# Row gathers of an expert layer: the added wait for a TensorE product taken away

## The chip, the cores and the metric

The kernel runs on one NeuronCore of a Trainium2 chip. The metric is the device time of one execution in microseconds (us), lower is better. Engines are named as in the profile: PE is TensorE (PEld its weight loads), DVE is VectorE, ACT is ScalarE, POOL is GpSimd, SP is SyncE, whose queue issues the plain loads and stores.

## The reference

The program is one layer of a sequence model on 512 tokens of width 2048. Retention and mLSTM mixing come first; the part that matters here is the last one, a "PEER" layer: each token picks 8 x 16 of 16384 experts, and an expert is one row of `peer_down` and one row of `peer_up`.

```
qh = (tb @ w_query).reshape(P_BLOCK, P_HEADS, 2, P_DQ // 2)
...
eid = jnp.take_along_axis(cand_i, best_j, axis=-1)
g = jax.nn.softmax(best_s, axis=-1)
act = jax.nn.gelu(jnp.einsum('thkd,td->thk', expert_down[eid], tb).astype(jnp.float32), approximate=False)
return jnp.einsum('thk,thkd->td', (g * act).astype(tb.dtype), expert_up[eid])
```

## The kernel before, in words

The expert layer is split by token. For 352 tokens (`ND`) it is computed densely on PE: every one of the 16384 experts, in 128 tiles of 128 experts. For the other 160 tokens (`G_` = 128 + 32) it is computed sparsely: rows of the two tables are gathered by index, and DVE multiplies them. The two run side by side in `experts`.

**The dense half.** A hidden tile (`hidden`, line 1187) is `dn[i]` times the activations: two weight loads of 512 KB, 16 products of three matmuls each (`mm3`, line 236; float32 is split into a high and a low part). The first 38 tiles (`NE`) were computed in earlier stages, stored to HBM as `hs` and come back as `hf`. A tile is multiplied by its gates (`gt`, line 1452) and split into high and low (`hh`, lines 233 and 234). Tiles form 16 groups of 8 (`GRP`); after a group, 16 weight loads of `upt` (line 1478 for the first output blocks, line 1494 for the others) give its share of the output (`part`, line 1468), which DVE adds into `acc` (line 1502). Each weight load, of `dn` or `upt`, goes through `weight` (line 224): one DMA into one of 7 `raw` buffers, a cast on ACT (line 228), a subtraction on DVE (line 229) into one of 3 `ws` buffers, and then exactly 24 matmuls of 352 columns. So the stage has 256 + 2 x 90 = 436 such weight steps.

**The sparse half.** There are 320 slots: 128 + 32 rows per token block from `dnr`, and then as many from `up`. `row` (line 1332) takes one slot: `rows` (line 1297) starts an indirect DMA from POOL's queue that gathers 128 rows of 2048 floats into one of three `row` buffers (`ROW_BUFS`), and the DVE operation of the slot two earlier (`LAG`) is emitted: `down` (line 1304, a product with a sum) or `up` (line 1310, multiply and add into `gacc`). `gather` (line 1325) calls `row` so that slots advance evenly with the PE work: `SPAN` is the total of all its arguments, and a slot is taken when its share has been reached.

**What sets the order.** The order in which `experts` emits work is only a priority. The framework's scheduler lays each engine's instructions out by priority and by when it expects their inputs to be ready, and on the chip each engine then runs its own list strictly in order. Weight steps are emitted with a raised priority (`AHEAD`). The gather has one dependency more than its data needs: `self.last` is the last matmul emitted so far, and `add_manual_dep` (line 1301) makes the gather wait for it.

```
            g = G.indirect_dma_start(out=r, out_offset=None, in_=src,
                                     in_offset=bass.IndirectOffsetOnAxis(ap=eid[i][:, s_:s_ + 1], axis=0))
            self.tc.add_manual_dep(g.ins, self.last.ins.name, PACE, reason="pace of the gathers")
```

Of the kernel before, what the change touches and what calls it, by code (L numbers as in the profile page):

```python
# [12 lines left out]
AF = mybir.ActivationFunctionType  # L13
OP = mybir.AluOpType
AX = mybir.AxisListType
PACE = mybir.DependencyInfo(mybir.DependencyClass.Sync, mybir.DependencyReason.DATA)
PSUM = bass.MemoryType.PSUM
DRAM = bass.MemoryType.DRAM

# [138 lines left out]
ND = T - G_  # L158
# [24 lines left out]
class K:  # L183
# [64 lines left out]
    def tjob(self, srcs, targets, nk=KT, order=range(8), one=False):  # L248

        n, last = 0, len(targets) - 1  # L250
        for u, src in enumerate(srcs):
            w = self.weight(src)
            for k8 in order if u else range(8):
                if n == self.LATE:
                    self.flush()
                if n in self.STEPS and self.mixing:
                    next(self.mixing, None)
                c = slice(k8 * P, (k8 + 1) * P)
                for t, (ps, rhs) in enumerate(targets):
                    self.last = self.mm3(ps, (w[:, 0, c], w[:, 1, c]), rhs(u * 8 + k8),  # L260
                                         n == 0 and not (one and t), n == nk - 1 and not (one and t < last))
                n += 1

# [1023 lines left out]
    def experts(self, d2):  # L1287
        a, V, S, TE, SY, G, d0 = self.a, self.V, self.S, self.TE, self.SY, self.G, self.d0
# [3 lines left out]
        eid = [self.eid[0].rearrange("p h k -> p (h k)"), self.eid[1]]  # L1292
# [3 lines left out]

        def rows(src, i, s_):
            r = d2.tile([P, D], F32, name="row", bufs=ROW_BUFS)
            g = G.indirect_dma_start(out=r, out_offset=None, in_=src,  # L1299
                                     in_offset=bass.IndirectOffsetOnAxis(ap=eid[i][:, s_:s_ + 1], axis=0))  # L1300
            self.tc.add_manual_dep(g.ins, self.last.ins.name, PACE, reason="pace of the gathers")
            return r

        def down(i, s_, r):
# [20 lines left out]
        def gather(n):  # L1325

            nonlocal done
            done += n
            while slots and NS - len(slots) < NS * done // SPAN:
                row()  # L1330

        def row():

            if slots:
                f, w, i, s_ = slots.pop(0)
                late.append((f, i, s_, rows(w, i, s_)))
            if len(late) > LAG or not slots:
                f, *x = late.pop(0)
                f(*x)
# [17 lines left out]
        def end0():  # L1357
            nonlocal xg, xh, sqg
            while slots or late:
                row()  # L1360
            t = d2.tile([P, 2, T], F32, name="xs", tag="gt", bufs=2)
            xh, sqg = t[:, 0].rearrange("p (k t) -> p k t", k=KT), t[:, 1]
            xg = d2.tile([P, KT, P], F32, name="xg", tag="row", bufs=ROW_BUFS)
            SY.dma_start(xg, self.X1[:, :, :P].rearrange("k p t -> p k t"))
            SY.dma_start(xh, self.X1[:, :, P:G_].rearrange("k p t -> p k t"))

        def end1():
            t = residuals(NPA)

            def more():  # L1370
                add_residuals(NPA, t)
                t2 = residuals(NPA + 4)
                self.todo.append(lambda: add_residuals(NPA + 4, t2))
            self.todo.append(more)
# [49 lines left out]
        def final(k, ps, x):  # L1424

            V.scalar_tensor_tensor(x2[k], ps[:, :ND], gt2[:, k:k + 1], x, op0=OP.mult, op1=OP.add)
            sq = d2.tile([P, ND], F32, name="sqd", bufs=2) if k else ssd[:, :ND]
            S.activation(sq, x2[k], AF.Square)
            if sqs:
                V.tensor_add(ssd[:, :ND], ssd[:, :ND], sqs.pop())  # L1430
            if k:
                sqs.append(sq)
# [3 lines left out]
        def tile(i):  # L1436

            g, j = divmod(i, 4)
            if j == 0:
                for n in range(len(gts), min(g + 2, P // 4)):  # L1440
                    gts[n] = d2.tile([P, ND // 32, 4, 32], F32, name="gt", bufs=2)
                    SY.dma_start(gts[n].rearrange("p c i t -> p c (i t)"), self.GD[n])
            if i < NE:
                t = d0.tile([P, ND], F32, name="hf", bufs=4)
                SY.dma_start(t, self.HS[i])
            else:
                self.todo.append(lambda: gather(HID // 2))
                t = self.hidden(i)
                gather(HID // 2)
            with self.tc.high_priority(offset=SOON):  # L1450
                tv = t.rearrange("p (c t) -> p c t", t=32)
                V.tensor_tensor(tv, tv, gts[g][:, :, j], OP.mult)
                w = d2.tile([P, 2, ND], F32R, name="hh", tag="hh", bufs=GRP + 1)
                self.split(w[:, 0], w[:, 1], t)
            return w

        hs = []
        for g in range(NG):
            for i in range(len(hs), min(GRP * (g + 1) + FORE, P)):
                if g == NG - 1 and i % GRP == GRP - 3:  # L1460
                    end0()
                    end1()
                elif g == NG - 1 and i % GRP == GRP - 1:
                    self.todo += [end3, end2]
                hs.append(tile(i))
            hh = hs[GRP * g:GRP * (g + 1)]

            def part(w, q, d_, ps, js):

                own = d_ >= NPA  # L1470
                for j in js:
                    c = slice(j * 256 + d_ % 2 * P, j * 256 + (d_ % 2 + 1) * P)
                    i = 4 * q + j
                    self.last = self.mm3(ps[:, :ND], (w[:, 0, c], w[:, 1, c]), (hh[i][:, 0], hh[i][:, 1]),
                                         i == 0 and (own or g == 0), i == GRP - 1 and (own or g == NG - 1))

            for q in range(GRP // 4):
                ws = [self.weight(a["upt"][g, u, q]) for u in range(NPA // 2)]
                for js in (range(3), (3,)) if g == NG - 1 and q == GRP // 4 - 1 else (range(4),):
                    for d_ in range(NPA):  # L1480
                        part(ws[d_ // 2], q, d_, pac[d_], js)
                gather((UP if (g + 1) * GRP > NE else UP0) * NPA // 2 * 4 // GRP)
            if g == NG - 1:
                for d_ in range(NPA):
                    x2[d_] = d0.tile([P, ND], F32, name="hf", bufs=4)
                    final(d_, pac[d_], xd[:, d_])
            for u in range(8):
                if g == NG - 1 and u in END:
                    (end4, end5)[END.index(u)]()
                if u >= NPA // 2:  # L1490
                    ds = (2 * u, 2 * u + 1)
                    pss = [self.ps("upp") for _ in ds]
                    for q in range(GRP // 4):
                        w = self.weight(a["upt"][g, u, q])
                        for d_, ps in zip(ds, pss):
                            part(w, q, d_, ps, range(4))
                            if q < GRP // 4 - 1:
                                continue
                            if g == 0:
                                V.tensor_copy(x2[d_], ps[:, :ND])  # L1500
                            elif g < NG - 1:
                                V.tensor_add(x2[d_], x2[d_], ps[:, :ND])
                            else:
                                final(d_, ps, x2[d_])
                    gather(UP if (g + 1) * GRP > NE else UP0)
        r = self.r2[:, :ND]
# [18 lines left out]
```

## Time and profile before

| | |
|---|---|
| median of 3 runs | 4090.67 us (4087.46 to 4096.19) |
| the profiled execution, its own time | 4075.81 us |
| its span in the trace | 4074.0 us |
| mean granted PE clock, share of full | 0.984 |
| bytes moved by DMA | 979.72 MB, mean 240 GB/s |
| of these by the gathers' queue | 335.56 MB |

Busy shares (PE 97%, DVE 70%, ACT 32%, POOL 11%) are means over the whole program; the dense and sparse halves of the experts run from about 2311 us to 4057 us, and that stretch has to be read by itself. A matmul's busy time overlaps its successor's, so the distance between the starts of two matmuls, not the duration of one, tells what PE needs. A wait is put down to the engine that came last. "DMA share" is the mean busy share of the core's 16 DMA engines.

### The profile page before, as it was taken

The page shows a single profiled execution, that of the slowest core. Times are in us where ns is not written, and L with a number is a line of the kernel's source. Part 1 is how long each engine was busy: PE and PEld are TensorE (multiplying, and loading weights), DVE is VectorE, ACT ScalarE, POOL GpSimd, SP SyncE. Part 2 cuts the span into 40 slices and gives each one's busy share as a digit, 9 for nine tenths or more (in the row PEclk, how much of TensorE's full clock was granted, in tenths as well). Part 3 has the DMA queues.
Part 4 walks back from the last instruction along what each step waited for, and adds up shares of the span by engine and source line. Part 5 has one row for each costly group of instructions (what it writes and reads, how often), then busy time and mean ns, then how long its engine had stood idle before and what let it go on. Part 6 is the DMA issues. An engine that isn't in the chain of part 4 may idle for free.

```text
span 4074.0 us, 56684 instructions
## 1 busy us (share of the span) xinstructions
PE 3950.5 (97%) x22470; PEld 3570.2 (88%) x22470; DVE 2860.3 (70%) x4448; ACT 1324.0 (32%) x1823; POOL 467.0 (11%) x328
## 2 busy tenths in 40 slices
PE   7999999999999999999999999999999999999998
PEld 4788887777788888799999999999999999999998
DVE  7952237677733443488889678888888888898956
ACT  3322124245422222343334333333223323333333
POOL 0000000000000000000000021333223333333300
PEclk7999999999999999999999999999999999999999
DMA  8522237667733444433357889999999999999963
GB/s 305 212 75 86 70 101 255 227 212 251 259 128 113 142 155 145 150 108 110 102 152 222 264 316 334 353 363 375 364 344 364 374 364 370 379 391 379 381 223 104
DMA packets 300539, 979.72 MB, mean 240 GB/s; under 512 B 32368, under 2 KB 101744, under 8 KB 259184
## 3 DMA queue, kind: packets, MB, share of 16 engines
q1 hardware_dynamic: 251888, 636.33, 45.7%
q0 software_dynamic: 46080, 335.56, 20.9%
q8 instruction: 176, 2.88, 0.3%
q10 hardware_dynamic: 2304, 4.20, 0.3%
q14 instruction: 91, 0.75, 0.1%
HBM read 915.63 MB, written 60.33 MB: 240 GB/s over the span
## 4 chain that ended last, share of the span: by engine, by line
PE 57%; DMA 20%; DVE 10%; issue 9%; ACT 1%; POOL 0%; SPq 0%; DVEq 0%; POOLq 0%; ACTq 0%
PE px L240 10%; PE px L238 10%; PE px L239 10%; DMA row<-in_dnr,eid 7%; DMA row<-in_up,eid 6%; PE hid L238 3%; DVE ws L229 3%; PE hid L240 3%; PE hid L239 3%; PE va L239 2%; PE va L238 2%; PE va L240 2%; DMA row<-in_dnr,eidx 2%; DVE gacc L1314 2%; DMA row<-in_up,eidx 2%
## 5 line engine op out<-in xcount | busy, mean ns | idle before, releaser
L229 DVE TENSOR_TENSOR ws<-raw,ws 128x1024 fp32r<-128x1024 f32 x770 | 937.0, 1220 | 608.1 <-ACT ws L228 606.5
L228 ACT CAST ws<-raw 128x1024 fp32r<-128x1024 f32 x770 | 805.6, 1049 | 1697.5 <-PE px L240 567.1
L240 PE MATMUL hid<-h,ws 128*128 128x352 f32 x2048 | 660.8, 323 | 23.5 <-DVE ws L229 23.3
L238 PE MATMUL hid<-h,ws 128*128 128x352 f32 x2048 | 674.5, 329 | 0.7 <-ACT ws L228 0.7
L239 PE MATMUL hid<-h,ws 128*128 128x352 f32 x2048 | 659.5, 322 | 0.0
L1299 POOL DMA_INDIRECT row<-in_dnr,eid x128 | 188.1, 1470 | 2777.6 <-DVE hh L234 2287.6
L238 PE MATMUL upp<-hh,ws 128*128 128x352 f32 x1536 | 499.2, 325 | 0.0
L240 PE MATMUL upp<-hh,ws 128*128 128x352 f32 x1536 | 493.0, 321 | 5.6 <-DVE ws L229 5.6
L239 PE MATMUL upp<-hh,ws 128*128 128x352 f32 x1536 | 493.7, 321 | 0.0
L1305 DVE SCALAR_TENSOR_TENSOR row<-row,h2n 128x2048 f32<-128x2048 f32 x160 | 365.7, 2289 | 92.2 <-DMA row<-in_dnr,eid 68.7
L1314 DVE SCALAR_TENSOR_TENSOR gacc<-row,wts,gacc 128x2048 f32<-128x2048 f32 x158 | 371.0, 2348 | 71.7 <-DMA row<-in_up,eid 56.2
L238 PE MATMUL px<-hhi,ws 128*128 128x512 f32 x1024 | 413.1, 403 | 0.0
L240 PEld LDWEIGHTS hid<-h,ws 128*128 128x128 f32 x2048 | 385.7, 188 | 31.0 <-DVE ws L229 30.7
L240 PE MATMUL px<-hhi,ws 128*128 128x512 f32 x1024 | 407.7, 398 | 0.0
L239 PE MATMUL px<-hlo,ws 128*128 128x512 f32 x1024 | 405.8, 396 | 0.0
L239 PEld LDWEIGHTS hid<-h,ws 128*128 128x128 f32 x2048 | 390.2, 191 | 0.0
L238 PEld LDWEIGHTS hid<-h,ws 128*128 128x128 f32 x2048 | 385.5, 188 | 0.9 <-ACT ws L228 0.9
L240 PEld LDWEIGHTS upp<-hh,ws 128*128 128x128 f32 x1536 | 288.8, 188 | 7.3 <-DVE ws L229 7.2
L239 PEld LDWEIGHTS upp<-hh,ws 128*128 128x128 f32 x1536 | 292.2, 190 | 0.0
L238 PEld LDWEIGHTS upp<-hh,ws 128*128 128x128 f32 x1536 | 288.3, 188 | 0.0
L240 PEld LDWEIGHTS px<-hhi,ws 128*128 128x128 f32 x1024 | 192.5, 188 | 48.1 <-issue 2.9
L239 PEld LDWEIGHTS px<-hlo,ws 128*128 128x128 f32 x1024 | 192.6, 188 | 43.6 <-issue 4.6
(451 smaller groups left out, 6474.5 us busy)
## 6 DMA issues: line engine op xcount, KB each, us to landing
raw<-in_dn SPq DMA_DIRECT2D x256, 512.0 KB
raw<-in_upt SPq DMA_DIRECT2D x256, 512.0 KB
raw<-in_wada_r SPq DMA_DIRECT2D x160, 512.0 KB
raw<-in_wt SPq DMA_DIRECT2D x130, 512.0 KB
gd<-sg SPq DMA_DIRECT2D x11, 2048.0 KB
gt<-gd SPq DMA_DIRECT2D x32, 704.0 KB
raw<-in_wada_s SPq DMA_DIRECT2D x32, 512.0 KB
raw<-in_wn SPq DMA_DIRECT2D x32, 512.0 KB
```

The lines of the kernel that those rows point to most:

```text
L228: self.S.copy(w[:, 0], r)
L229: self.V.tensor_sub(w[:, 1], r, w[:, 0].bitcast(F32))
L238: mm(out, lhsT=l[0], rhs=r[0], start=start, stop=False)
L239: mm(out, lhsT=l[0], rhs=r[1], start=False, stop=False)
L240: return mm(out, lhsT=l[1], rhs=r[0], start=False, stop=stop)
L1299: g = G.indirect_dma_start(out=r, out_offset=None, in_=src, in_offset=bass.IndirectOffsetOnAxis(ap=eid[i][:, s_:s_ + 1], axis=0))
L1305: V.scalar_tensor_tensor(r, r, 1.0, self.h2n[i], op0=OP.mult, op1=OP.mult, accum_out=dots[i][:, s_:s_ + 1])
L1314: V.scalar_tensor_tensor(gacc[i], r, wts[i][:, s_:s_ + 1], gacc[i], op0=OP.mult, op1=OP.add)
```

## The change

The argument that named the last matmul goes, and with it the gather's extra dependency. A gather still waits for its buffer, that is for the DVE operation that read it three slots before.

```
-PACE = mybir.DependencyInfo(mybir.DependencyClass.Sync, mybir.DependencyReason.DATA)
...
-                    self.last = self.mm3(ps, (w[:, 0, c], w[:, 1, c]), rhs(u * 8 + k8),
+                    self.mm3(ps, (w[:, 0, c], w[:, 1, c]), rhs(u * 8 + k8),
...
-            g = G.indirect_dma_start(out=r, out_offset=None, in_=src,
-                                     in_offset=bass.IndirectOffsetOnAxis(ap=eid[i][:, s_:s_ + 1], axis=0))
-            self.tc.add_manual_dep(g.ins, self.last.ins.name, PACE, reason="pace of the gathers")
+            G.indirect_dma_start(out=r, out_offset=None, in_=src,
+                                 in_offset=bass.IndirectOffsetOnAxis(ap=eid[i][:, s_:s_ + 1], axis=0))
...
-                    self.last = self.mm3(ps[:, :ND], (w[:, 0, c], w[:, 1, c]), (hh[i][:, 0], hh[i][:, 1]),
+                    self.mm3(ps[:, :ND], (w[:, 0, c], w[:, 1, c]), (hh[i][:, 0], hh[i][:, 1]),
```

Lines after the removed ones stand one or two numbers lower in the changed kernel (229 becomes 228, 1305 becomes 1303, 1502 becomes 1500).

The first place is POOL's own queue in the stage, which holds nothing but gathers. Before, with the semaphores each waits for (DMASW is the queue's own count, DVE the buffer, PE the product):

```order
L1299 DMA row<-in_dnr,eid 128x2048 [waits DMASW5_49,DVE_49,PE_49]
L1299 DMA row<-in_dnr,eid 128x2048 [waits DMASW6_49,DVE_49,PE_49]
L1299 DMA row<-in_dnr,eid 128x2048 [waits DMASW7_49,DVE_49,PE_49]
L1299 DMA row<-in_dnr,eid 128x2048 [waits DMASW0_49,DVE_49,PE_49]
L1299 DMA row<-in_dnr,eid 128x2048 [waits DMASW1_49,DVE_49,PE_49]
```

The same place now:

```order
L1298 DMA row<-in_dnr,eid 128x2048 [waits DMASW5_49,DVE_49]
L1298 DMA row<-in_dnr,eid 128x2048 [waits DMASW6_49,DVE_49]
L1298 DMA row<-in_dnr,eid 128x2048 [waits DMASW7_49,DVE_49]
L1298 DMA row<-in_dnr,eid 128x2048 [waits DMASW0_49,DVE_49]
L1298 DMA row<-in_dnr,eid 128x2048 [waits DMASW1_49,DVE_49]
```

The wait for PE is gone, the order of the gathers is the same. The second place is DVE's list in the second group's `upt` part. Here `ws` is a weight step, `row,dots` the operation that reads a gathered row, and `acc` the addition of a result of PE. Before:

```order
L229 TENSOR_TENSOR ws<-raw,ws 128x1024 x2
L1502 TENSOR_TENSOR acc<-acc,upp 128x352
L1305 SCALAR_TENSOR_TENSOR row,dots_18631<-row,h2n_11759 128x2048
L1502 TENSOR_TENSOR acc<-acc,upp 128x352
L229 TENSOR_TENSOR ws<-raw,ws 128x1024 x2
L1502 TENSOR_TENSOR acc<-acc,upp 128x352
L1305 SCALAR_TENSOR_TENSOR row,dots_18631<-row,h2n_11759 128x2048
L1502 TENSOR_TENSOR acc<-acc,upp 128x352
```

The same part now:

```order
L1303 SCALAR_TENSOR_TENSOR row,dots_18631<-row,h2n_11759 128x2048
L228 TENSOR_TENSOR ws<-raw,ws 128x1024
L1500 TENSOR_TENSOR acc<-acc,upp 128x352
L1303 SCALAR_TENSOR_TENSOR row,dots_18631<-row,h2n_11759 128x2048
L228 TENSOR_TENSOR ws<-raw,ws 128x1024
L1500 TENSOR_TENSOR acc<-acc,upp 128x352
L1303 SCALAR_TENSOR_TENSOR row,dots_18631<-row,h2n_11759 128x2048
L228 TENSOR_TENSOR ws<-raw,ws 128x1024
```

Where one row operation stood to two weight steps, one stands to each. Counted over DVE's whole list of the stage: the 320th and last row operation stood behind weight step 394 of 436, and now stands behind weight step 320; 100 tiles of `hf` and `hh` and 144 operations on `acc` lie ahead of it, where 121 and 168 did. The third place is the start of the stage on DVE. Before:

```order
L1422 MEMSET ssd 128x32
L229 TENSOR_TENSOR ws<-raw,ws 128x1024 x3
L1452 TENSOR_TENSOR hf<-hf,gt 128x352
L234 TENSOR_TENSOR hh<-hf,hh 128x352
L1452 TENSOR_TENSOR hf<-hf,gt 128x352 x2
```

The same place now:

```order
L1420 MEMSET ssd 128x32
L228 TENSOR_TENSOR ws<-raw,ws 128x1024
L1303 SCALAR_TENSOR_TENSOR row,dots_18631<-row,h2n_11759 128x2048
L228 TENSOR_TENSOR ws<-raw,ws 128x1024
L1303 SCALAR_TENSOR_TENSOR row,dots_18631<-row,h2n_11759 128x2048
L228 TENSOR_TENSOR ws<-raw,ws 128x1024
L1303 SCALAR_TENSOR_TENSOR row,dots_18631<-row,h2n_11759 128x2048
L1450 TENSOR_TENSOR hf<-hf,gt 128x352 x3
L233 TENSOR_TENSOR hh<-hf,hh 128x352 x3
```

Three row operations now stand ahead of the first `hf` and `hh`. PE's list differs only in the first group's first `part`, whose products come in another order; SP's list has the same transfers, some of them a few places earlier or later.

## Rows read from the trace of the kernel before

**Rows 1.** The page: busy time, share and count; DMA share in 40 slices.

```profile
PE 3950.5 (97%) x22470; PEld 3570.2 (88%) x22470; DVE 2860.3 (70%) x4448; ACT 1324.0 (32%) x1823; POOL 467.0 (11%) x328
...
DMA  8522237667733444433357889999999999999963
```

**Rows 2.** Timeline of PE at the stage's first and last matmuls: start us, us, instruction.

```profile
2311.29 0.66 PE L238 MATMUL pac<-hh,ws 128*128 128x352 f32 x1 [6.03 <-ACT hh L233]
...
4056.75 0.32 PE L239 MATMUL upp<-hh,ws 128*128 128x352 f32 x1
4056.91 0.32 PE L240 MATMUL upp<-hh,ws 128*128 128x352 f32 x1
```

**Rows 3.** Windows: stretch, length; busy PE, PEld, DVE, ACT, POOL; clock, DMA share, GB/s.

```profile
2300.00:2600.00 300.00, 293.32 (x1810) 291.86 (x1810) 231.52 (x282) 97.83 (x120) 63.34 (x40) 0.98 0.87 322
2600.00:3900.00 1300.00, 1260.15 (x7745) 1248.51 (x7745) 1135.13 (x1013) 398.09 (x485) 399.22 (x280) 0.99 0.96 371
```

**Rows 4.** Waits from 2320 us on: engine, line, releaser: total us, times, longest.

```profile
POOL row L1299 <- PE upp L240: 350.0, 71, 8.7
POOL row L1299 <- PE hid L240: 177.6, 62, 7.7
POOL row L1299 <- PE pac L240: 176.5, 27, 10.9
POOL row L1299 <- DVE gacc L1314: 131.7, 42, 6.3
...
PE hid L240 <- DVE ws L229: 22.7, 18, 4.0
...
PE pac L240 <- DVE ws L229: 11.7, 9, 3.3
```

**Rows 5.** The page: the gathers' queue, and sizes of the loads.

```profile
q0 software_dynamic: 46080, 335.56, 20.9%
...
raw<-in_upt SPq DMA_DIRECT2D x256, 512.0 KB
...
gt<-gd SPq DMA_DIRECT2D x32, 704.0 KB
...
hf<-hs SPq DMA_DIRECT2D x38, 176.0 KB
```

**Rows 6.** Windows of 50 us, columns as in group 3.

```profile
2700.00:2750.00 50.00, 45.63 (x268) 45.06 (x267) 38.69 (x40) 13.44 (x16) 14.86 (x9) 0.93 0.88 330
...
3350.00:3400.00 50.00, 48.73 (x305) 48.45 (x304) 45.24 (x35) 15.99 (x20) 13.13 (x10) 1.00 0.99 395
...
3650.00:3700.00 50.00, 50.00 (x315) 50.00 (x314) 47.92 (x38) 14.63 (x16) 14.96 (x13) 1.00 0.99 386
```

**Rows 7.** DVE's groups, 2311 to 3890 us: busy us, mean ns; idle before, releasers.

```profile
L229 DVE TENSOR_TENSOR ws<-raw,ws 128x1024 fp32r<-128x1024 f32 x393 | 476.9, 1219 | 31.9 <-ACT ws L228 30.9 <-issue 0.8
L1314 DVE SCALAR_TENSOR_TENSOR gacc<-row,wts,gacc 128x2048 f32<-128x2048 f32 x158 | 371.0, 2348 | 71.7 <-DMA row<-in_up,eid 56.2 <-DMA row<-in_up,eidx 14.6
L1305 DVE SCALAR_TENSOR_TENSOR row<-row,h2n 128x2048 f32<-128x2048 f32 x160 | 365.7, 2289 | 92.2 <-DMA row<-in_dnr,eid 68.7 <-DMA row<-in_dnr,eidx 22.7
L1502 DVE TENSOR_TENSOR acc<-acc,upp 128x352 f32<-128x352 f32 x156 | 80.1, 513 | 0.0
L234 DVE TENSOR_TENSOR hh<-hf,hh 128x352 fp32r<-128x352 f32 x121 | 61.6, 518 | 4.3 <-ACT hh L233 4.0
```

**Rows 8.** Timelines of POOL and DVE: first gather, its product, and the last product.

```profile
2323.21 2.89 POOL L1299 DMA_INDIRECT row<-in_dnr,eid  x1 [2282.44 <-DVE hh L234]
...
2333.74 2.29 DVE L1305 SCALAR_TENSOR_TENSOR row<-row,h2n 128x2048 f32<-128x2048 f32 x1 [3.38 <-DMA row<-in_dnr,eid]
...
3886.46 2.35 DVE L1314 SCALAR_TENSOR_TENSOR gacc<-row,wts,gacc 128x2048 f32<-128x2048 f32 x1 [1.04 <-DMA row<-in_up,eidx]
```

**Rows 9.** Timeline of PE behind a wait for a row, at the lower clock.

```profile
2723.56 0.50 PE L238 MATMUL pac<-hh,ws 128*128 128x352 f32 x1
2723.85 0.50 PE L239 MATMUL pac<-hh,ws 128*128 128x352 f32 x1
```

## The prediction

> **What bounds the kernel now.** Read the page first: PE is busy 97% of the span, and DMA stands at 8 or 9 tenths from slice 23 of 40 (2241 us) to the last but two [rows 1]. Two resources are nearly full at the same time there, so the expert stage has to be taken by itself. Its first dense matmul starts at 2311.29 us, its last at 4056.91 us [rows 2]: 1745.6 us. Two matmuls start 0.160 us apart at the higher clock level [rows 2], a weight step has 24 of them, so PE needs 24 x 0.160 = 3.84 us for a step and 436 x 3.84 = 1674.2 us for all. The stage loses 71.4 us to gaps and to the lower clock level, and that is all that any change of the gathers can win in it.
>
> Where do those gaps come from? In the table of waits PE waits for `ws` of DVE (22.7 us and 11.7 us) [rows 4], and DVE, which runs its list in order, waits for rows that have not landed (71.7 us before `gacc`, 92.2 us before the products with `h2n`) [rows 7]. POOL on its side waits for PE 350.0 + 177.6 + 176.5 = 704.1 us in 160 waits, 4.4 us each [rows 4]. So there is something to win in principle: a gather that starts 4.4 us earlier would be there in time.
>
> But the transfers are the other limit. DMA moved 371 GB/s at a share of 0.96 over the 1300 us from 2600 us on, against 322 GB/s in the 300 us before [rows 3]. In windows of 50 us with a share of 0.99 it was 395 and 386 GB/s [rows 6]. No row shows more.
>
> **The bytes now.** A gather moves 335.56 MB / 320 = 1.049 MB [rows 5]; a weight step 512 KB = 0.524 MB; a `gt` 0.721 MB, an `hf` 0.180 MB [rows 5]. Up to the last row operation, behind weight step 394, that is 335.6 + 394 x 0.524 + 32 x 0.721 + 38 x 0.180 = 572 MB, and it stood at 3886.46 us [rows 8], 1575 us after the start: 363 GB/s. At 386 GB/s these bytes need 1482 us; PE needs 394 x 3.84 = 1513 us for the same steps. Spread like this, the transfers just fit under PE.
>
> **The change, part by part.**
>
> *The wait.* 704.1 us of POOL's waiting go [rows 4]. POOL itself does nothing with the time; what ends later is the wait for the buffer, which already ended last 42 times in `gacc`'s stretch (131.7 us) [rows 4]. No instruction is added. Queued behind a gather on POOL there are only gathers.
>
> *The order.* The scheduler, freed of the wait, puts one row operation to each weight step where it had put one to two at first. This is the costly part. The row operations are 320 as before, but now behind 320 weight steps, not 394. The bytes up to there: 335.6 + 320 x 0.524 + 27 x 0.721 + 38 x 0.180 = 529.7 MB (27 `gt`: 100 tiles in fours, and two ahead). PE needs 320 x 3.84 = 1229 us for these steps. The transfers need 529.7 / 386 = 1372 us. DVE's list puts the row operation ahead of the next `ws`, so when a row is late the weights are late, and PE waits.
>
> *DVE.* Up to the same point it has 320 x 1.219 + 160 x 2.289 + 160 x 2.348 + 144 x 0.513 + 200 x 0.518 = 1309 us [rows 7]. Neighbours overlap a little: before, the same five kinds and `hf` (121 like `hh`) sum to 476.9 + 371.0 + 365.7 + 80.1 + 2 x 61.6 = 1417 us, and the busy time was 231.52 + 1135.13 = 1367 us [rows 3], a factor of 0.965. So DVE needs 1263 us: above PE, below DMA. It is not the bound, but with 92% of the DMA's time it has little to catch up with.
>
> *The rest.* Once the rows are through, 116 weight steps are left, and nothing but their weights is moved: 116 x 3.84 = 445 us. What PE lost earlier can't be won back there, because PE is then the bound at its own pace.
>
> *The start.* Three row operations now precede the first `hh`. Before, from issue to product the first gather took 2333.74 - 2323.21 = 10.5 us [rows 8]. If PE stood for that long with nothing moving, it would cost 10.5 us. The transfers run meanwhile, so this is inside the sum for DMA, and I take 0; PE's new order in the first `part` costs nothing either, since the same products wait for the same `hh`.
>
> **The sum.** 1372 + 445 - 1745.6 = +71 us. The tail behind the last matmul (17 us of the span) stays. On the profiled execution's own 4075.81 us that is 4147 us; the median of the runs shown lies 14.9 us higher, and I count from it: 4090.67 + 71 = **4162 us**.
>
> The unknown term is the rate. The nearest row is 386 GB/s: there, 13 gathers started in 50 us beside 13 weight steps [rows 6], the mix that the change makes the rule. Its bounds: 395 GB/s (1341 us, +41 us: 4131 us), and the mean of the paced stretch with its holes, 371 GB/s (1428 us, +128 us: 4219 us). It can be that low because DVE's list still has places where `hf`, `hh` and `acc` crowd together; three buffers then fill and the gathers pause.
>
> The Trainium skill gives rates too. "DMA: Bandwidth & Descriptors", Specifications, has a fabric ceiling of 435 GB/s for a core, and a limit of 358 GB/s for its share of HBM. As estimates from that page, the bytes above would need 1218 us by the first, under PE's need, so that the change would cost nothing; by the second 1480 us, +179 us. The rows contradict the second (395 GB/s) and none of them reaches the first; the measured rates decide.
>
> **The rivals.**
>
> *Faster: the deeper queue moves more.* Up to three gathers are now always under way, and the DMA engines never wait for PE. The rate at which the change breaks even is 529.7 / (1745.6 - 445) = 407 GB/s, 3% over the best window [rows 6]. Above 529.7 / 1263 = 419 GB/s DVE would be the bound: 1263 + 445 - 1745.6 = -38 us, 4053 us. For it: the share was 0.96, not 1 [rows 3]. Against it: at a share of 0.99 the rate is 386 to 395. The Trainium skill's ceiling of 435 GB/s, above, is the case for this rival. Chance 0.10.
>
> *No change: the wait was a formality.* If the buffer came free about when PE released the gather, the gathers would start as before: 4091 us. For it: the 131.7 us in which the buffer ended last [rows 4]. Against it: 704.1 us for PE, and an order on DVE that really is another. Chance 0.06.
>
> *Much slower: the clock.* Where DVE waited for a row at 2718 us, PE stood, and was then granted the lower level (1.2 GHz): matmuls 0.293 us apart [rows 9], 7.03 us for a step, a granted clock of 0.93 over that window [rows 6]. With DMA as the bound, a step takes 1372 / 320 = 4.29 us, and PE has 0.45 us to spare in each. That hides the lower level as long as at most 23% of the stretch is at it, a granted clock of about 0.88; below that the clock decides. At 0.80 (40% at the lower level) a step takes 4.69 us: 1502 + 445 - 1745.6 = +201 us, 4292 us. For it: every step now has a stall. Against it: in the paced stretch the clock was 0.99 [rows 3], and short stalls in one window of 48.73 us busy left it at 1.00 [rows 6]. The Trainium skill ("TensorE: Matmul & The Clock Gate", HAM oscillation) tells of kernels whose PE idles briefly between batches and pays the clock's fall each time; by that rule this rival is the likelier one. Chance 0.10.
>
> **How the numbers follow.** The forecast, rates from 371 to 395 GB/s, has 0.70; the rivals 0.10, 0.06 and 0.10; 0.04 is left for a loss between 8 and 41 us. A measurement tells about 0.2% (8 us) from no change. So faster 0.10, same 0.06, slower 0.84. The range from 4090 to 4225 us takes in the bounds of the rate, the small losses and half of "no change"; it leaves out the faster rival, the other half and most of the clock's rival, together just under 0.2.
>
> **What would show it.** Right: the gathers' POOL waits name DVE alone; in the windows up to about 3700 us the DMA share is 0.97 or more and GB/s between 371 and 395, with PE busy some 90%; the waits of PE for `ws` and of DVE for rows grow several times; the last row operation ends near 2311 + 1372 = 3683 us, about 200 us earlier than now, and PE is full from there to the end. Wrong: more than 407 GB/s over hundreds of us; or PE busy above 95% there; or a granted clock below 0.88.

## The result and the profile after

| | before | changed |
|---|---|---|
| median | 4089.07 us (6 runs, 4078.57 to 4096.19) | 4161.99 us (6 runs, 4153.1 to 4165.73) |
| profiled execution, own time | 4075.81 us | 4163.27 us |
| span in the trace | 4074.0 us | 4161.2 us |

The ratio is 1.0178, with a 95% interval of 1.0161 to 1.0195: slower by 1.8%, 73 us between the medians. The profiled executions lie 87 us apart, since that of before was 13 us quicker than its median.

The windows of the changed kernel, in the columns of [rows 3] (stretch, length, busy time of PE, PEld, DVE, ACT and POOL, clock, DMA share, GB/s):

```profile
2300.00:2600.00 300.00, 264.33 (x1558) 259.04 (x1557) 251.06 (x292) 84.15 (x102) 89.35 (x57) 0.93 0.95 361
2600.00:3650.00 1050.00, 987.53 (x5927) 962.72 (x5927) 953.76 (x827) 302.44 (x371) 412.15 (x253) 0.98 0.98 387
...
3700.00:4130.00 430.00, 430.00 (x2706) 429.95 (x2705) 204.61 (x265) 147.29 (x182) 0.00 (x0) 1.00 0.46 146
```

Against [rows 3], DMA went from 322 to 361 GB/s at the start and from 371 to 387 GB/s behind it, with PE busy 88% and 94% of these stretches where it had been 98% and 97%. From 3700 us on PE is full, and the DMA engines have half their time free. The counts tell the same as the order: 253 gathers in 1050 us, one to 4.15 us, where there were 280 in 1300 us, one to 4.64 us.

PE's timeline at the stage's ends, and DVE's at the last row operation:

```profile
2325.11 0.95 PE L237 MATMUL pac<-hh,ws 128*128 128x352 f32 x2 [17.48 <-ACT hh L232]
```
```profile
4144.22 0.32 PE L239 MATMUL upp<-hh,ws 128*128 128x352 f32 x1
```
```profile
3689.60 2.35 DVE L1312 SCALAR_TENSOR_TENSOR gacc<-row,wts,gacc 128x2048 f32<-128x2048 f32 x1 [0.16 <-DMA row<-in_up,eidx]
```

The rows are through at 3690 us, 197 us earlier than in [rows 8], and the stage ends 87 us later than in [rows 2]. From the first matmul to the last row operation it takes 1364 us, from there to the end 455 us.

The waits from 2320 us on, as in [rows 4]:

```profile
POOL row L1298 <- DVE row L1303: 451.8, 151, 16.9
...
POOL row L1298 <- DVE gacc L1312: 380.6, 148, 5.2
...
DVE gacc L1312 <- DMA row<-in_up,eid: 47.5, 58, 2.9
...
DVE row L1303 <- DMA row<-in_dnr,eid: 36.1, 45, 4.0
DVE hf L1450 <- DMA hf<-hs: 34.3, 10, 11.8
PE hid L239 <- DVE ws L228: 32.8, 35, 3.9
PE upp L239 <- DVE ws L228: 32.3, 17, 5.1
```

POOL waits almost only for its buffers, 832 us in all. PE's waits for `ws` in the `hid` tiles rose from 22.7 to 32.8 us, and the `upp` blocks stand beside them with 32.3 us. DVE, though, waits for rows less than it did: 47.5 us where [rows 7] have 56.2 us, and 36.1 us where they have 68.7 us. So the gathers do come earlier, and DVE is busier: 954 of 1050 us, 91%, where it was busy 1135 of 1300 us, 87% [rows 3]. Whether the transfers or DVE hold the stage, these rows do not settle; the experiments have to.

### The profile page after: what moved, and what is told of

The parts are those of the page before. It is cut to its first block, busy times and chain, and to the rows that moved or that the text cites. A ratio compares the mean times of both kernels' runs of the same rounds, so it can differ in the third digit from the quotient of the medians.

```text
span 4161.2 us, 56736 instructions
## 1 busy us (share of the span) xinstructions
PE 3982.7 (96%) x22470; PEld 3582.8 (86%) x22470; DVE 2866.4 (69%) x4448; ACT 1323.5 (32%) x1823; POOL 522.6 (13%) x328
## 4 chain that ended last, share of the span: by engine, by line
PE 59%; DMA 13%; issue 13%; DVE 7%; POOL 6%; ACT 1%; SPq 0%; POOLq 0%; DVEq 0%; ACTq 0%
PE px L237 10%; PE px L239 10%; PE px L238 10%; DMA row<-in_up,eid 8%; POOL row L1298 6%; PE hid L237 4%; PE hid L239 4%; PE hid L238 4%; DVE gacc L1312 3%; PE va L237 2%; PE va L238 2%; PE va L239 2%; DMA row<-in_up,eidx 2%; PE upp L237 1%; PE upp L238 1%
## 5 line engine op out<-in xcount | busy, mean ns | idle before, releaser
L1298 POOL DMA_INDIRECT row<-in_dnr,eid x128 | 206.2, 1611 | 2637.0 <-DMA raw<-in_upt 2244.2
L239 PE MATMUL upp<-hh,ws 128*128 128x352 f32 x1536 | 501.5, 326 | 32.9 <-DVE ws L228 32.3
L237 PE MATMUL upp<-hh,ws 128*128 128x352 f32 x1536 | 503.8, 328 | 0.0
L238 PE MATMUL upp<-hh,ws 128*128 128x352 f32 x1536 | 498.3, 324 | 0.0
L1312 DVE SCALAR_TENSOR_TENSOR gacc<-row,wts,gacc 128x2048 f32<-128x2048 f32 x158 | 371.3, 2350 | 59.8 <-DMA row<-in_up,eid 47.5
L1303 DVE SCALAR_TENSOR_TENSOR row<-row,h2n 128x2048 f32<-128x2048 f32 x160 | 366.1, 2290 | 49.2 <-DMA row<-in_dnr,eid 36.1
L239 PEld LDWEIGHTS upp<-hh,ws 128*128 128x128 f32 x1536 | 292.9, 191 | 41.7 <-DVE ws L228 41.3
L238 PEld LDWEIGHTS upp<-hh,ws 128*128 128x128 f32 x1536 | 296.0, 193 | 0.0
L237 PEld LDWEIGHTS upp<-hh,ws 128*128 128x128 f32 x1536 | 292.6, 191 | 0.0
L1298 POOL DMA_INDIRECT row<-in_up,eid x128 | 206.1, 1610 | 328.3 <-DVE gacc L1312 302.1
```

What stands on the lines that cost most here:

```text
L237: mm(out, lhsT=l[0], rhs=r[0], start=start, stop=False)
L238: mm(out, lhsT=l[0], rhs=r[1], start=False, stop=False)
L239: return mm(out, lhsT=l[1], rhs=r[0], start=False, stop=stop)
L1298: G.indirect_dma_start(out=r, out_offset=None, in_=src, in_offset=bass.IndirectOffsetOnAxis(ap=eid[i][:, s_:s_ + 1], axis=0))
L1303: V.scalar_tensor_tensor(r, r, 1.0, self.h2n[i], op0=OP.mult, op1=OP.mult, accum_out=dots[i][:, s_:s_ + 1])
L1312: V.scalar_tensor_tensor(gacc[i], r, wts[i][:, s_:s_ + 1], gacc[i], op0=OP.mult, op1=OP.add)
```

## The experiments

The theory behind the forecast was: removing the wait lets the scheduler pack the row operations denser, one to a weight step, and the transfers then can't keep up at 386 to 395 GB/s. The rivals: the missing wait itself, DVE's in-order list, and the start of the stage. Ratios are to the kernel before in runs on the same chip.

### The missing wait without the new order

```
-PACE = mybir.DependencyInfo(mybir.DependencyClass.Sync, mybir.DependencyReason.DATA)
+PACE = mybir.DependencyInfo(mybir.DependencyClass.NoSync, mybir.DependencyReason.DATA)
```

A dependency of this class is seen by the scheduler and leaves no semaphore on the chip.

> The kernel before, but the dependency on the last product is one for the scheduler alone: the order on every engine stays nearly that of before (the 320th row operation stands behind weight step 393 on DVE, before it was 394), and on the chip a gather waits for its buffer alone. If the loss comes from the denser order and the transfers that it asks for (theory), this has none of it: the bytes up to the last row operation need 572 MB / 386 GB/s = 1482 us and PE 393 x 3.84 = 1509 us, so 4050 to 4095 us. If the loss comes from the missing wait on the chip itself, by gathers that start at once and crowd out the weights (rival), it is as slow as the change: 4140 to 4180 us.

Measured: 4035.82 us, ratio 0.9895 (0.9879 to 0.9912). That is faster than before, 14 us below the theory's range, and 2.8% faster than the change (1.0178 / 0.9895). So the missing wait is not what makes the change slow. A window of this kernel:

```profile
2600.00:3200.00 600.00, 597.36 (x3728) 595.99 (x3726) 538.55 (x547) 193.21 (x231) 220.99 (x135) 1.00 0.97 383
```

Behind 2600 us PE is busy 597 of 600 us. What the wait cost is now to be seen: a gather that starts as soon as its buffer is free raises DMA to 383 GB/s (364 GB/s in the same 600 us of the kernel before), and PE's stalls there are nearly gone. So the change has two halves: the wait's end gains 1.05%, and the order that comes with it loses it again and 1.8% more. What the wait costs in the dense order was not measured.

### The density alone

The same kernel, with slots taken faster:

```
-            while slots and NS - len(slots) < NS * done // SPAN:
+            while slots and NS - len(slots) < NS * done // int(SPAN * 0.81):
```

> The kernel of the first experiment (the old dependency kept for the scheduler alone), with slots taken faster: the divisor is 0.81 of the total. The order is as even as in the kernel before, but the last row operation stands behind weight step 329 instead of 393, and the first hh still ahead of the first row operation. If density alone makes the loss (theory): 335.6 + 329 x 0.524 + 27 = 535 MB, 1386 us at 386 GB/s, then 107 x 3.84 = 411 us; 1797 - 1745.6 = +51 us against before: 4120 to 4160 us. If it is something else in the changed kernel's order, such as its start (rival), this stays with the first experiment: 4030 to 4065 us.

Measured: 4155.52 us, ratio 1.0175 (1.0145 to 1.0204), that of the change (1.0178). Its window shows the change's rate too:

```profile
2600.00:3200.00 600.00, 553.74 (x3315) 541.60 (x3314) 538.88 (x520) 168.48 (x205) 229.58 (x146) 0.97 0.99 387
```

With 0.90 in place of 0.81:

> As the kernel with 0.81, with 0.90: the last row operation stands behind weight step 358. Theory (transfers as the bound): 335.6 + 358 x 0.524 + 28 = 551 MB, 1428 us at 386 GB/s, then 78 x 3.84 = 300 us; 1728 - 1745.6 = -18 us, and a few us of stalls as in the first experiment: 4060 to 4085 us, between the first experiment and the dense kernels. Rival (a threshold: at any density above before's the queue collapses): 4120 us or more.

Measured: 4089.63 us, ratio 1.0019 (1.0001 to 1.0038), 5 us over the expectation's upper end, and no collapse. So the density makes the loss, and step by step: last row operation behind weight step 393, 358 and 329: ratio 0.9895, 1.0019 and 1.0175. From 393 to 358 a step costs 54 us / 35 = 1.5 us, from 358 to 329 66 us / 29 = 2.3 us; the theory's rate for a stage bound by transfers was 3.84 - 0.524 MB / 386 GB/s = 2.5 us a step. The price does not hold further: the changed kernel, with its last row operation 9 steps earlier, behind 320, should by it be some 21 us slower than the one with 329, and it has the same ratio. Why is not shown.

### Half the bytes

The changed kernel with tables cut to 1024 columns, and each row operation done as two on that half:

```
-    a["up"] = f(up)
+    a["up"] = f(up[:, :D // 2])
...
-            V.scalar_tensor_tensor(r, r, 1.0, self.h2n[i], op0=OP.mult, op1=OP.mult, accum_out=dots[i][:, s_:s_ + 1])
+            for h in (self.h2n[i][:, D // 2:], self.h2n[i][:, :D // 2]):
+                V.scalar_tensor_tensor(r[:, :D // 2], r[:, :D // 2], 1.0, h, op0=OP.mult, op1=OP.mult, accum_out=dots[i][:, s_:s_ + 1])
```

(and the same for `dnr` and for `up`; the gather writes `r[:, :D // 2]`).

> The changed kernel with tables cut to their first 1024 columns: a gather moves half the bytes, and each row operation is done as two of 1024 elements on that half, so DVE has the same elements to do (the second half of each row is left out of the result). The order stays dense: the last row operation stands behind weight step 332. If the transfers are the bound (theory), it goes: bytes up to there 168 + 332 x 0.524 + 27 = 369 MB, 956 us at 386 GB/s, under PE's 1275 us; what is left is DVE at about 1300 us, 1300 + 104 x 3.84 - 1745.6 = -46 us, and some stall at the start: 4040 to 4090 us. If DVE's in-order list with one row operation to each weight step is the bound (rival), it stays at 4140 us or above.

Measured: 4101.47 us, ratio 1.0059 (1.0036 to 1.0082). Neither: a good part of the loss goes, but the time stays over the theory's 4090 us. The order is a little less dense than the change's (332 against 320), but the dense kernel with 329 has the change's ratio, so the order is not what was gained. The windows say why it stays over:

```profile
2600.00:3200.00 600.00, 564.87 (x3406) 548.23 (x3405) 549.19 (x750) 172.41 (x212) 218.91 (x143) 0.99 0.76 259
3200.00:3600.00 400.00, 394.25 (x2442) 390.25 (x2441) 389.59 (x388) 122.14 (x150) 177.31 (x98) 1.00 0.79 274
```

DMA has a quarter of its time free, and DVE is busy 549 of 600 us and 390 of 400 us. With the transfers out of the way DVE is the bound. Its groups in this kernel show that it also had more to do than in the change, because of the splitting:

```profile
L1315 DVE SCALAR_TENSOR_TENSOR gacc<-row,wts,gacc 128x1024 f32<-128x1024 f32 x315 | 393.8, 1276 | 18.4 <-DMA row<-in_up,eid 13.6 <-DMA row<-in_up,eidx 4.6
L1304 DVE SCALAR_TENSOR_TENSOR row<-row,h2n 128x1024 f32<-128x1024 f32 x314 | 378.9, 1219 | 57.1 <-DMA row<-in_dnr,eid 42.9 <-DMA row<-in_dnr,eidx 14.0
```

For 640 halves that is some 787 us, against 320 x 2.32 = 742 us for the whole operations of [rows 7]. So DVE had some 45 us more to do, and half the bytes without this extra work would have taken off the 49 us or more.

### Half the products

The dense kernel with 0.81, with row operations on half of a full row:

```
-            V.scalar_tensor_tensor(r, r, 1.0, self.h2n[i], op0=OP.mult, op1=OP.mult, accum_out=dots[i][:, s_:s_ + 1])
+            V.scalar_tensor_tensor(r[:, :D // 2], r[:, :D // 2], 1.0, self.h2n[i][:, :D // 2], op0=OP.mult, op1=OP.mult, accum_out=dots[i][:, s_:s_ + 1])
```

> The same, with row operations on the first 1024 elements alone (the second half of each row is left out of the result): nearly the same order (last row operation behind weight step 325) and the same bytes, but DVE has some 370 us less to do. If the transfers are the bound at this density (theory), it gains little: 533 MB at 391 GB/s, 1363 us, and 111 x 3.84 = 426 us; +44 us against before: 4105 to 4140 us. If DVE's in-order list is the bound (rival), PE's 1674 us for the stage come within reach: 4020 to 4060 us.

Measured: 4106.73 us, ratio 1.0056 (1.0036 to 1.0075): inside the theory's range, yet 49 us off the dense order, more than it can explain at the 391 GB/s it assumed. The windows:

```profile
2600.00:3200.00 600.00, 574.20 (x3491) 569.80 (x3491) 413.71 (x544) 174.85 (x212) 233.24 (x156) 0.98 1.01 411
3200.00:3600.00 400.00, 379.93 (x2304) 376.18 (x2303) 278.21 (x285) 117.32 (x144) 158.04 (x105) 0.97 1.01 410
```

411 GB/s at a share of 1.01. So the 386 to 395 GB/s of [rows 6] were not the transfers' limit.

The same edit in the changed kernel as it is lets the scheduler pack denser still:

> The changed kernel with full gathers, but row operations on the first 1024 elements alone (the second half of each row is left out of the result): DVE's work on rows is halved, the bytes are the same. The scheduler then packs the rows denser still: the last row operation stands behind weight step 266. If the transfers are the bound (theory), less work makes it slower: 335.6 + 266 x 0.524 + 24 = 499 MB, 1293 us at 386 GB/s, then 170 x 3.84 = 653 us, 1946 - 1745.6 = +200 us: 4240 to 4300 us. If DVE is the bound (rival), its sum falls by some 370 us and the time falls below the change's, to 4100 us or less.

Measured: 4250.65 us, ratio 1.042 (1.0397 to 1.0444): with DVE's work on rows halved the kernel is slower, as the theory had it. DVE is busy 390 of 600 us, and from 2600 to 3600 us it waits 326 us for rows:

```profile
2600.00:3200.00 600.00, 531.45 (x3078) 519.97 (x3078) 390.23 (x500) 154.96 (x189) 213.58 (x155) 0.94 0.99 394
```

So DVE's work is not the bound here, and the rows' coming is. But 394 GB/s is no limit of the transfers either, since the kernel above moved 411. Both issue a gather every 3.9 us (155 and 156 in 600 us); what is less here is the weights beside them (3078 matmuls against 3491). PE's lower granted clock (0.94) may have a part in it; that was not tried.

### Both halves

The dense kernel with 0.81, with the row operations of "Half the products" and the tables and the gather of "Half the bytes", whose line for the gather is:

```
-            g = G.indirect_dma_start(out=r, out_offset=None, in_=src,
+            g = G.indirect_dma_start(out=r[:, :D // 2], out_offset=None, in_=src,
```

> The dense order once more (last row operation behind weight step 324), with tables of half the width and row operations on that half alone, so both bytes and DVE's work on rows are halved (the second half of each row is left out of the result). Halving the bytes alone took 49 us off the dense order, halving the products alone 49 us too. If these two, each close to its limit, make the whole loss (theory), nothing but PE is left: a stage of 1690 to 1710 us and 4015 to 4045 us. If a third cause is there, such as the place of the row operations in DVE's list or the clock (rival), 4070 us or more is left.

Measured: 4017.35 us, ratio 0.9837 (0.9816 to 0.9859). The dense order is harmless when both are light:

```profile
2600.00:3200.00 600.00, 600.00 (x3752) 600.00 (x3751) 452.86 (x577) 197.02 (x236) 231.22 (x171) 1.00 0.85 297
```

Either half alone took 1.2% off, both together 3.4%. Two limits lie close to each other; taking one away leaves the other. PE is busy all of the 600 us, so no third cause shows there.

### A fourth row buffer

The dense kernel with 0.81; `raw` buffers go from 7 to 5 to make room, and the control has that alone:

```
-RAW_BUFS, WS_BUFS = 7, 3
+RAW_BUFS, WS_BUFS = 5, 3
...
-ROW_BUFS = 3
+ROW_BUFS = 4
```

> The dense order (last row operation behind weight step 329) with four row buffers instead of three, and five raw buffers instead of seven to make room. Theory (DVE and the transfers hold each other up through three buffers, so neither reaches its limit): with a fourth the transfers come from 375 GB/s towards the 395 to 410 that the half products showed: 1302 to 1355 us + 411 us, -32 to +20 us against before: 4070 to 4120 us. Rival (the transfers' own limit under this mix): as its control with three buffers.

> The control for four row buffers: the same order with three row buffers and five raw buffers. Theory and rival: as the dense kernel with seven, 4150 to 4165 us, or some 10 to 30 us slower where fewer weights are loaded ahead.

Measured: 4100.39 us, ratio 1.0049 (1.003 to 1.0069), with four row buffers; 4173.42 us, ratio 1.0214 (1.0191 to 1.0236), in the control. The order of the row operations against the weight steps is the same in both. The windows, first with four, then the control's:

```profile
2600.00:3200.00 600.00, 582.14 (x3583) 578.83 (x3582) 577.99 (x556) 185.56 (x222) 243.50 (x157) 0.99 1.02 416
3200.00:3600.00 400.00, 373.15 (x2286) 371.04 (x2285) 386.67 (x287) 118.57 (x143) 147.44 (x106) 0.97 1.02 415
```
```profile
2600.00:3200.00 600.00, 553.60 (x3298) 542.09 (x3297) 535.57 (x522) 169.41 (x209) 231.78 (x145) 0.97 0.98 386
```

One buffer more, and DMA goes from 386 to 416 GB/s, DVE from 536 to 578 of 600 us. With three buffers each holds the other up: a gather can't start while DVE is late, and DVE can't go on while a row is late. The times bear it out, as an estimate: in the changed kernel a gather lands 9.3 to 9.6 us after its issue (medians of its trace), and its row operation takes 2.3 us, so a buffer is taken for 11.6 us or more, and three buffers allow a gather every 3.9 us at best; the windows of the change have one every 4.15 us. With four buffers a gather takes 11.1 to 11.9 us to land, but DVE's waits for rows from 2600 to 3600 us fall from 85 us in the control to 26 us. What is left, 1.5% over the first experiment's 0.9895, has both close to full: a DMA share of 1.02, and DVE busy 96%.

### The start

The changed kernel with the old dependency for its first 8 gathers, in the scheduler alone (`NoSync`, as above):

```
+            if i == 0 and s_ < 8 and src is a["dnr"]:
+                self.tc.add_manual_dep(g.ins, self.last.ins.name, PACE, reason="pace of the gathers")
```

> The changed kernel with the first 8 gathers placed by the old dependency (for the scheduler alone), so that the first group's hf and hh stand ahead of the first row operation again. The changed kernel's first dense matmul starts at 2325 us, before it was 2311 us. The last row operation stands behind weight step 330. Theory: the start's 14 us come back, and 10 steps less density give 10 x 2.5 = 25 us: 4115 to 4150 us. Rival (the start is hidden, since the transfers go on meanwhile, and only their sum counts): 4137 to 4165 us.

Measured: 4153.11 us, ratio 1.018 (1.0157 to 1.0203): no gain. Of the theory's 39 us, 14 for the start and 25 for ten steps less density, none came back. The first gathers were still issued at 2291 us, and DVE waited for the first `hf`:

```profile
2322.99 0.53 DVE L1453 TENSOR_TENSOR hf<-hf,gt 128x352 f32<-128x352 f32 x1 [6.56 <-DMA hf<-hs]
```

With the old order at the start the first `hf` is still late, so the order is not what delayed it. With the wait kept on the chip for the first three gathers:

```
+            if i == 0 and s_ < 3 and src is a["dnr"]:
+                self.tc.add_manual_dep(g.ins, self.last.ins.name, PACE, reason="pace of the gathers")
```

> The changed kernel with the old wait, on the chip too, for the first three gathers alone: the dense order (last row operation behind weight step 327), the first hh ahead of the first row operation, and no gather beside the first hf loads. It differs from the kernel with the start held in its order by that wait alone, in the main. Theory (early gathers delay the first hf, and with them the whole stage): the first dense matmul comes within 4 to 5 us of the last weight step's subtraction again, and the time falls by 6 to 14 us: 4138 to 4148 us, ratio to before 1.014 to 1.0165. Rival (once rows and DVE bound the stage, what moves at the start is hidden): no change, ratio 1.017 to 1.019.

Measured: 4159.85 us, ratio 1.0184 (1.0159 to 1.0208). The rival holds, though this interval of some 10 us either way can't exclude a gain of a few us. The first `hf` came in time again:

```profile
2318.54 0.53 DVE L1453 TENSOR_TENSOR hf<-hf,gt 128x352 f32<-128x352 f32 x1 [2.49 <-DMA hf<-hs]
```

In the dense order no gain shows, which fits a stage in which rows and DVE, not PE, decide what follows. Where PE decides, it may count; the first experiment's kernel with this wait (`PLACE` is its dependency without a semaphore, `PACE` the old one):

```
-            self.tc.add_manual_dep(g.ins, self.last.ins.name, PACE, reason="pace of the gathers")
+            self.tc.add_manual_dep(g.ins, self.last.ins.name, PACE if i == 0 and s_ < 3 and src is a["dnr"] else PLACE, reason="pace of the gathers")
```

> The first experiment's kernel, with the old wait on the chip kept for the first three gathers. There the first gathers were issued at 2285 us, beside the first hf and gt loads, and hf landed 7.7 us behind the last weight step's subtraction instead of 3.8 us. Theory: these 4 us and up to 4 more come back: 4024 to 4034 us, the best so far. Rival (the start is noise): 4034 to 4040 us.

Measured: 4022.45 us, ratio 0.986 (0.9837 to 0.9884), against 0.9895 (0.9879 to 0.9912) without. That is 2 us under the theory's range. The intervals overlap a little, so the size of this gain is not settled. It is the fastest kernel of this study with the whole computation, 1.4% faster than before:

```profile
2600.00:3200.00 600.00, 599.72 (x3748) 599.23 (x3747) 546.59 (x553) 195.71 (x236) 229.63 (x137) 1.00 0.97 385
```

## Why the prediction was right

4162 us was forecast and 4161.99 us measured. That agreement is closer than its steps deserve.

**The order.** One row operation to a weight step, the last behind step 320: the density alone gives the whole ratio (1.0175 against 1.0178). This step was right, and it is the one that carries the forecast. That the wait's end by itself gains 1.05% was not in the sum.

**The rate.** 386 GB/s was taken, 387 GB/s measured over 1050 us. The size was right, its reason only half. That the transfers are at their limit there ("the transfers are the other limit") fell: with a fourth buffer the same mix ran at 416 GB/s. The rate is what transfers and DVE reach together over three buffers. In this the "faster" rival was right about the DMA engines, whose break-even of 407 GB/s they can pass, and wrong about the change, which doesn't let them. Of the Trainium skill's two figures ("DMA: Bandwidth & Descriptors", Specifications) the trace leaves the 435 GB/s standing (416 GB/s measured); the 358 GB/s is passed by every dense kernel with whole rows.

**DVE.** "It is not the bound": the size was right, the reading was not. 1263 us of work were forecast up to the last row operation, and 1229 us were measured, 90% of the 1364 us. Against 1372 us for DMA that looked like room. In the kernel with half the bytes DVE was busy 390 of 400 us, and halving its products as well took another 2.2% off (1.0059 to 0.9837). So DVE binds together with the transfers, and not behind them.

**A sign that failed.** By "when a row is late the weights are late, and PE waits" the prediction wanted PE's waits for `ws` and DVE's for rows to "grow several times". PE's grew from 40 to 71 us, less than twice. DVE's fell, from 162 to 107 us. The other signs held: the gathers wait for DVE, DMA had a share of 0.98 at 387 GB/s (only the first 300 us fell short, with 0.95 and 361 GB/s), PE was busy 94%, the rows were through at 3690 us and PE was full from there. The number is the sum's, but its picture, DVE idle for rows that the transfers bring too slowly, is only half of what happened.

**What could be won.** The bound of 71.4 us for the gain was not passed: the largest gain, with both halves taken away, was 1.6%, some 65 us. The 704.1 us of waiting for PE ([rows 4]) were worth 1.05% when taken away alone. Taken away with the order, they were outweighed.

**The sum.** From the first matmul to the last row operation 1364 us were measured where the sum had 1372 us; behind it 455 us, not 445 us; and the stage began 14 us late. On the profiled executions this is +87 us, not +71 us. Against the medians it is +73 us, since the profiled execution of before was 13 us quicker than usual. About 15 us of the exact agreement are therefore luck. The 1364 us hide two errors that cancel in part: from the first matmul to the last row operation DMA moved 381 GB/s, not 386, and some 520 MB, not 529.7, part of it because six gathers (6.3 MB) had been issued before.

**The start.** 0 was taken, with 10.5 us as the upper bound. The first matmul came 13.8 us later, beyond that bound. The first gathers were issued 38 us earlier than in [rows 8], beside the loads of the first `hf`:

```profile
2284.79 1.38 POOL L1298 DMA_INDIRECT row<-in_dnr,eid  x1 [2244.18 <-DMA raw<-in_upt]
```

With the wait kept for three gathers the first `hf` came 4 us earlier than without, and the time did not fall beyond the noise. So 0 was right within some 10 us.

**The clock.** Granted 0.98 over 1050 us, 0.93 in the first 300 us: above the 0.88 at which, by the prediction's sum, it would have decided. The Trainium skill's rule on short idle times ("TensorE: Matmul & The Clock Gate", HAM oscillation) would have made it the likelier case; here the lower level stayed rare. What it took of the 73 us was not tried separately.

## What to carry to other kernels

A dependency between engines does two things, it makes the chip wait and it tells the scheduler when to place what; here the first cost 1.05% and the second was worth 2.8% (measured without the wait), so they should be tried separately. Row work that is packed to the front of a stage loads DMA and DVE there and leaves both idle behind it, while PE can't catch up; spread it until the slowest engine's pace fits. Two resources at 90 to 98% joined by few buffers bound each other at less than either's limit, and relieving one of them shows only part of the loss.

## What was not expected of the hardware

Gathers of 8 KB rows beside 512 KB weight loads ran at 410 to 416 GB/s over 1000 us (shares of 1.01 and 1.02), 4 to 5% over the best window of [rows 6]. And halving DVE's work on rows made the changed kernel 2.4% slower (1.042 against 1.0178), since for a lighter DVE the scheduler packed the rows denser (the last behind step 266 in place of 320); in an order that was nearly held, the same halving made it 1.2% faster.
